# Streaming the two halves of split float32 activations as one 512-column matmul

## The chip, the cores and the metric

The kernel runs on one core of a Trainium2 chip, in one launch. The metric is the device time of that core in microseconds (us), lower is better. Three runs of the kernel before took 940.13 to 944.43 us, with a median of 941.47.

## The reference

Two layers of a decoder trunk on x of shape (1, 256, 1024), all float32. Each layer is, cut to what matters here:

```
xn = rms(x);  z = xn @ w_in                  # 1024 -> 7756 columns, split among the mixers and the gates
y_a = mlstm(silu(conv(z.mqk)), ...)          # 4 heads x 128, chunks of 128
y_b = dsa(top 64 of an indexer's scores)     # 8 heads x 64
y_c = diff_attn(...)                         # 4 heads x 128, two softmax maps
gates = sigmoid(z.g + b_gate)                # 3 x 1024
m = sum_b gates[b] * (y_b @ w_branch[b])     # 512 -> 1024, three times
x = x + m @ w_out                            # 1024 -> 1024
g, u = split(rms(x) @ w_gate_up)             # 1024 -> 2 x 2816
x = x + (silu(g) * u) @ w_down               # 2816 -> 1024
```

Every projection has to be as exact as float32 nearly is, so each float32 operand is split into a high part (rounded to the format that TensorE takes in one pass, float32r) and a low part (the rest). A product is then three passes: high x high, high x low and low x high.

## The kernel before

The 256 tokens are the columns of nearly everything. The weights of a layer are read in 151 chunks of at most 128 x 1024 numbers, in the fixed order of `plan()`: mLSTM q and k, the latent, the indexer, then queries, keys and values of the attentions and the mLSTM (512 columns each), 24 blocks of gates, 12 chunks of the branches, 8 of the output projection, 44 of gate and up, and 24 of the down projection. `chunk` (line 472) brings one in: a DMA into `raw`, a ScalarE copy into `whi` (the high part), a VectorE subtraction into `wlo` (the low part); each of the three has 3 buffers.

Two helpers multiply. `feat` (line 490) gives features as rows and the 256 tokens as columns: its stationary operand is a 128 x 128 block of weights, its moving operand the activations. An activation tile `a` is 128 x 2 x 256: `a[:, 0, :]` is the high part and `a[:, 1, :]` the low part, next to each other. Three matmuls of 256 columns follow each other: high weights with high activations, high weights with low activations, low weights with high activations. `tok` (line 497) gives tokens as rows; its moving operand is 256, 332 or 512 columns of weights. The change does not touch `tok`.

`feat` serves the mLSTM q and k (line 676, activations `xg`), the gates (line 1002, `xg`), the branches (line 1019, `y`), the output projection (line 1042, `mg`), gate and up (line 1052, `fx`) and down (line 1067, `h`). Its results go to tiles called `mm`, of which 4 exist, each one PSUM bank (2 KB per partition, 512 float32). A bank holds two groups of 256 columns side by side (two feature blocks) in the mLSTM, the gates, the branches and gate and up, and one group in the output and down projections. VectorE takes them out in one instruction, times 1/rms (`rB`), times the gate, or added to x.

The order of the work is not that of the code. `Order` records every instruction, and `schedule` puts them in an order by a list schedule: each engine takes the instruction that can start first, and among those of one time the one with the lowest number (its place in the code, less what `early` gives). `cost` (line 319) says how long an instruction lasts. Two instructions that touch one PSUM tile depend on each other even where they touch different halves, unless both only read. Each engine then runs its list strictly in that order, so a wait holds up all behind it. All instructions are issued at line 288, so the profile shows only that line and one has to go by the names of tiles. `K` is a tile of constants, `at` are the PSUM tiles of the attentions (4 more banks), `pad`, `cv` and `mqk` belong to the convolution, `gt` are gates, `mu` the gated branches, `gr` and `hf` the two halves of the feed-forward part, `dn` the down projection.

Of the kernel before, what the change touches and what calls it, by code (L numbers as in the profile page):

```python
# [11 lines left out]
F32 = mybir.dt.float32  # L12
# [7 lines left out]
class View:  # L20
    """A tile that is allocated when its first instruction is issued, or a part of it."""
# [96 lines left out]
class Order:  # L118
    """Records instructions, puts them in an order by a list schedule, and issues them in it."""
# [187 lines left out]
def lat(a, b):  # L307
    """From the end of an instruction on engine a to the start of one on b that reads it, in us."""
    if a == b:
        return {"tensor": 0.0, "vector": 0.127, "scalar": 0.15, "gpsimd": 0.13, "sync": 0.0}[a]  # L310
    if b == "tensor":
        return 0.25
    return 0.2 if a == "tensor" or "gpsimd" in (a, b) else 0.14
# [5 lines left out]
def cost(op, views):  # L319
    """The time of an instruction in us."""  # L320
    n = max(math.prod(v.shape[1:]) for v in views)
    psum = any(v.base.psum for v in views)
    if op.eng == "tensor":
        n = math.prod(views[0].shape[1:])
        if op.fn == "transpose":
            return 0.109
        if views[1].dtype == BF16:
            return n / 1200
        if views[1].dtype == F32R:
            return max(n, 256) / 2400 + 0.0024  # L330
        return 0.216 if n <= 128 else 4 * n / 2400 + 0.0048
    if op.eng == "scalar":
        t = (0.05 if psum else 0.092) + n * 0.00084
        extra = [op.kw.get("scale"), op.kw.get("bias"), op.kw.get("accum_out")]
        return t + 0.093 * sum(isinstance(v, View) for v in extra)
    if op.eng == "vector":
        if op.fn == "reciprocal":
            return 0.05 + n * 0.0063
        t = 0.065 + n * (0.00052 if op.fn in ("tensor_copy", "tensor_scalar") and not psum else 0.00104)
        if op.fn == "scalar_tensor_tensor":  # L340
            t += 0.061 * isinstance(op.args[2], View)
        if op.fn == "tensor_tensor_reduce":
            t += 0.061 * isinstance(op.args[3], View)
        if op.fn == "tensor_scalar":
            t += 0.061 * sum(isinstance(v, View) for v in op.args[2:4])
        return t
    if op.eng == "gpsimd":
        if op.kw.get("op") == OP.pow:
            return 0.3 + n * 0.165
        if op.fn == "memset":  # L350
            return 0.04 + n * 0.0005
        if op.fn in ("tensor_scalar", "tensor_copy"):
            return 0.16 + n * (0.0037 if any(isinstance(v, View) for v in op.args[2:4]) else 0.00083)
        return 0.15 + n * 0.0021
    return 0.02 + 128 * n * 4 / 365e3
# [26 lines left out]
def plan():  # L382
    """The order in which a layer's weights are read: (array, row blocks, col blocks)."""
    seq = []
    for f in range(8):
        seq.append([("in", k, O_QK + f * 128, 128) for k in range(8)])
    for a in range(2):
        seq.append([("in", k, O_CKV, 256) for k in range(4 * a, 4 * a + 4)])
    for ks in ((0, 1, 2), (3, 4, 5), (6, 7)):
        seq.append([p for k in ks for p in (("in", k, O_IQ, 324), ("in", k, O_IF, 8))])  # L390
    for a in range(4):
        seq.append([("in", k, O_SQ, 512) for k in (2 * a, 2 * a + 1)])
    for a in range(2):
        seq.append([("kv", k, 512 * a, 512) for k in range(2)])
    for o in (O_DQ, O_DK, O_DV, O_MV, O_MO):
        for a in range(4):
            seq.append([("in", k, o, 512) for k in (2 * a, 2 * a + 1)])
    for g in range(24):
        seq.append([("in", k, O_G + g * 128, 128) for k in range(8)])
    for b in BR:  # L400
        for ep in range(4):
            seq.append([("br%d" % b, k, ep * 256, 256) for k in range(4)])
    for e in range(8):
        seq.append([("out", k, e * 128, 128) for k in range(8)])
    for f in range(NFF):
        seq.append([("gu", k, f * 128, 128) for k in range(8)])
        seq.append([("gu", k, FF + f * 128, 128) for k in range(8)])
    for e in range(8):
        for ks in (range(0, 8), range(8, 16), range(16, 22)):
            seq.append([("dn", k, e * 128, 128) for k in ks])  # L410
    return seq
# [8 lines left out]
def kernel(ctx: ExitStack, tc: tile.TileContext, xT: bass.AP, wts: bass.AP, cst: bass.AP,  # L420
# [33 lines left out]
    # keeps TensorE's clock up until the first operands are there  # L454
# [35 lines left out]
    def feat(ps, w, c0, a, first, last):  # L490
        """ps [128 out, T] += w[:, c0:c0+128]^T a, three passes."""
        hi, lo = w
        PE.matmul(ps, hi[:, c0:c0 + 128], a[:, 0, :], start=first, stop=False)
        PE.matmul(ps, hi[:, c0:c0 + 128], a[:, 1, :], start=False, stop=False)
        PE.matmul(ps, lo[:, c0:c0 + 128], a[:, 0, :], start=False, stop=last)

    def tok(ps, w, c0, n, a, t, first, last):
        """ps [128 tok, n] += a[:, :, tile t]^T w[:, c0:c0+n], three passes."""
# [6 lines left out]
    def rsqrt_cols(t, n):  # L505
        """t <- t ** -0.5 on GpSimd (t [128, n])."""
        G.tensor_tensor(t, t, mhalf[:, :n], op=OP.pow)

    def norm(gcol, wide, first=False):
        """x*g as hi/lo parts, 1/rms as token columns [128, 2] and as rows [128, T]."""  # L510
# [63 lines left out]
    def swap_halves(ap):  # L574
        """[128, h, 64] seen with the halves of the last axis exchanged, as two views."""
        return ap[:, :, 32:64], ap[:, :, 0:32]

    def rot(dst, z, nh, a, b):
        """dst = z * a + swap(z) * b over nh heads; a, b [128, 64]."""
# [16 lines left out]
    def qk_heads(z, t, ab, dstT, query):  # L596
        """z [128 tok, 512] -> per-head RMS, RoPE, transposed into dstT[:, :, tile t]. Of a query
        the 1/rms is returned instead, as columns scaled by -1/sqrt(64), for softmax."""
# [20 lines left out]
    def softmax(t, heads, qT, kT, bias, scale):  # L619
        """exp(logits - max) of the heads, [128 q, len(heads), nk], and its row sums."""  # L620
# [16 lines left out]
    def keyT(p, n, t):  # L637
        """p [128 q, n, nk] -> [128 keys, n, key tile, 128 q]."""
# [8 lines left out]
    def parts(dst, ps, t, g=None):  # L647
        """hi/lo of ps [128, 4, 128] (scaled by g[:, k]) into dst[:, k, :, tile t]."""
# [11 lines left out]
    for li in range(L):  # L660
# [13 lines left out]
        # mLSTM q and k: projection, causal convolution, silu  # L674
        mqk = []
        for fp in range(4):
            ps = mmps([128, 2, T])
            for j in range(2):
                w = w_first if li == 0 and fp + j == 0 else chunk(li)
                for k in range(8):  # L680
                    feat(ps[:, j, :], w, k * 128, xg[k], k == 0, k == 7)
            qk = S.tile([128, 2, T], F32, tag="mqk", name="mqk", bufs=4)
            for j in range(2):
                f = 2 * fp + j
                pad = pads[j]
                with S.early(400):
                    V.tensor_mul(pad[:, 3:3 + T], ps[:, j, :], rB)
# [8 lines left out]
        # DSA latent  # L696
# [30 lines left out]
        # indexer projections and mLSTM gates  # L727
# [28 lines left out]
        # index scores and the top-k mask  # L756
# [25 lines left out]
        # DSA queries  # L782
# [15 lines left out]
        # DSA keys and values  # L798
# [15 lines left out]
        # DSA attention  # L814
# [19 lines left out]
        # differential attention  # L834
# [62 lines left out]
        # mLSTM gates  # L897
# [48 lines left out]
        # (s tile, t tile) blocks: (0, 0), (1, 1), (0, 1)  # L946
# [7 lines left out]
        # mLSTM values and output gate  # L954
# [44 lines left out]
        # branch gates  # L999
        gt = []  # L1000
        S.margin = MG
        for gp in range(12):
            ps = mmps([128, 2, T])
            for j in range(2):
                w = chunk(li)
                for k in range(8):
                    feat(ps[:, j, :], w, k * 128, xg[k], k == 0, k == 7)
            g = S.tile([128, 516], F32, tag="h", name="gt", bufs=22)[:, :512].rearrange("p (a t) -> p a t", a=2)
            with S.early(400):
                V.tensor_mul(g, ps, rB[:, None, :].to_broadcast([128, 2, T]))  # L1010
# [5 lines left out]
        # branch projections, gated and merged  # L1016
        mg = []
        us = [None] * 4
        for n, b in enumerate(BR):
            for ep in range(4):  # L1020
                w = chunk(li)
                ps = mmps([128, 2, T])
                for j in range(2):
                    for k in range(4):
                        feat(ps[:, j, :], w, k * 256 + j * 128, y[b][:, k], k == 0, k == 3)
                u = tmp([128, 2, T], "mu")
                V.scalar_tensor_tensor(u, gt[4 * b + ep], 1.0, ps, op0=OP.add, op1=OP.mult)
# [13 lines left out]
        # output projection  # L1041
        for e in range(8):
            w = chunk(li)
            ps = mmps([128, T])
            for k in range(8):
                feat(ps, w, k * 128, mg[k], k == 0, k == 7)
            V.tensor_add(x[e], x[e], ps)

        # SwiGLU
        xg, rcol, rB = norm(c[:, C_NF:C_NF + 8], True)  # L1050
        hs = []
        for f in range(NFF):
            ps = mmps([128, 2, T])
            for j in range(2):
                w = chunk(li)
                for k in range(8):
                    feat(ps[:, j, :], w, k * 128, xg[k], k == 0, k == 7)
            gr = tmp([128, T], "gr")
            V.tensor_mul(gr, ps[:, 0, :], rB)
            A.activation(gr, gr, AF.Silu)  # L1060
            hf = tmp([128, T], "hf")
            V.tensor_mul(hf, gr, ps[:, 1, :])
# [4 lines left out]
        for e in range(8):  # L1067
            ps = mmps([128, T])
# [5 lines left out]
            V.tensor_mul(d, ps, rB)  # L1074
# [26 lines left out]
def _layout(inp):  # L1101
    """The inputs in the kernel's layouts (moves only)."""
# [43 lines left out]
```

## Time and profile before

| | |
|---|---|
| runs, median (lowest to highest) | 941.47 us (940.13 to 944.43) |
| the profiled execution, first to last instruction | 942.7 us |
| matmuls | 7154 |
| HBM read | 158.27 MB, 169 GB/s over the span |

The page names no other time of the profiled execution than its span, which lies within the runs. An engine's busy share is an average over stages of very different kind; 16 DMA engines were busy for about half the span. Ends of matmuls are modelled: starts are what can be trusted.

### The profile page before, as it was taken

How to read it: one execution, taken by the hardware profiler on the slowest of the kernel's cores; microseconds unless marked ns; L12 is line 12 of the kernel's file. 1: busy time of each engine (PE TensorE's matmuls, PEld its weight loads, DVE VectorE, ACT ScalarE, POOL GpSimd, SP SyncE). 2: the span in 40 equal slices, each digit the busy share in tenths (PEclk: the TensorE clock that was granted, in tenths of full speed). 3: DMA queues.
4: the chain of work that ended last, by engine and by line, in shares of the span. 5: the costliest groups of instructions: out<-in, count | busy, mean ns of one | idle time of the engine just before them, and what ended most of it. 6: DMA issues, size and time to landing. Idle time of an engine off the chain costs nothing.

```text
span 942.7 us, 18057 instructions
## 1 busy us (share of the span) xinstructions
PE 933.5 (99%) x7154; PEld 888.6 (94%) x7154; DVE 678.6 (72%) x1268; ACT 534.0 (57%) x927; POOL 103.3 (11%) x149
## 2 busy tenths in 40 slices
PE   8999999999999999999999999999999999999998
PEld 7988779999999999999999787899999999999998
DVE  6889988765886666665578898796669866666553
ACT  5686667774365444444457767577644655445432
POOL 5002431110011000001110121213000300000000
PEclk9999999999999999999999999999999999999999
DMA  6655433445555555555555453333555555555663
GB/s 222 203 188 179 154 100 106 131 163 187 186 179 181 189 191 181 188 181 186 186 184 184 157 193 121 112 113 118 176 187 192 178 180 185 194 181 186 193 198 96
DMA packets 46821, 160.49 MB, mean 170 GB/s; under 512 B 5392, under 2 KB 7568, under 8 KB 46736
## 3 DMA queue, kind: packets, MB, share of 16 engines
q1 hardware_dynamic: 46736, 159.34, 52.0%
q8 instruction: 56, 0.92, 0.4%
q14 instruction: 29, 0.24, 0.1%
HBM read 158.27 MB, written 1.05 MB: 169 GB/s over the span
## 4 chain that ended last, share of the span: by engine, by line
PE 98%; DVE 1%; DMA 0%; issue 0%; SPq 0%; ACT 0%
PE mm L288 89%; PE at L288 8%; DVE e L288 0%; DMA x<-in_xT_dram 0%; DVE xg L288 0%; SPq L288 0%; DVE zr L288 0%; ACT xg L288 0%; DVE dn L288 0%; DVE x L288 0%; DVE rot L288 0%; ACT nsq L288 0%; DVE wlo L288 0%; DVE mn L288 0%; DVE cf L288 0%
## 5 line engine op out<-in xcount | busy, mean ns | idle before, releaser
L288 ACT ACTIVATE whi<-raw 128x1024 fp32r<-128x1024 f32 (+2 forms) x303 | 315.9, 1043 | 332.9 <-PE mm L288 212.0
L288 DVE TENSOR_TENSOR wlo<-raw,whi 128x1024 fp32r<-128x1024 f32 (+2 forms) x303 | 365.4, 1207 | 184.0 <-ACT whi L288 182.2
L288 PE MATMUL mm<-fx,whi 128*128 128x256 f32 x1408 | 249.6, 279 | 0.0
L288 PEld LDWEIGHTS mm<-fx,whi 128*128 128x128 f32 x1408 | 215.2, 188 | 0.0
L288 PE MATMUL mm<-xg,whi 128*128 128x256 f32 x1024 | 195.2, 289 | 1.8 <-DVE xg L288 1.8
L288 PE MATMUL mm<-fx,wlo 128*128 128x256 f32 x704 | 196.8, 280 | 0.0
L288 PEld LDWEIGHTS mm<-xg,whi 128*128 128x128 f32 x1024 | 163.7, 195 | 3.3 <-DVE xg L288 2.6
L288 PE MATMUL mm<-whi,xg 128*128 128x512 f32 (+2 forms) x512 | 150.3, 373 | 0.0
L288 PE MATMUL mm<-xg,wlo 128*128 128x256 f32 x512 | 148.0, 289 | 0.6 <-DVE wlo L288 0.6
L288 PEld LDWEIGHTS mm<-fx,wlo 128*128 128x128 f32 x704 | 132.0, 188 | 0.0
L288 PE MATMUL mm<-h,whi 128*128 128x256 f32 x704 | 124.5, 280 | 0.0
L288 PEld LDWEIGHTS mm<-h,whi 128*128 128x128 f32 x704 | 107.7, 188 | 0.0
L288 PEld LDWEIGHTS mm<-whi,xg 128*128 128x128 f32 x512 | 92.1, 188 | 14.7 <-issue 1.0
L288 PEld LDWEIGHTS mm<-xg,wlo 128*128 128x128 f32 x512 | 99.7, 195 | 1.2 <-DVE wlo L288 0.9
L288 PE MATMUL mm<-h,wlo 128*128 128x256 f32 x352 | 98.6, 280 | 0.0
L288 PE MATMUL mm<-wlo,xg 128*128 128x512 f32 (+2 forms) x256 | 95.6, 374 | 0.0
L288 PE MATMUL mm<-y,whi 128*128 128x256 f32 x384 | 67.9, 280 | 0.0
L288 PEld LDWEIGHTS mm<-h,wlo 128*128 128x128 f32 x352 | 66.4, 189 | 0.0
L288 POOL TENSOR_TENSOR nacc<-nacc,nsq 128x256 f32<-128x256 f32 x28 | 26.3, 939 | 361.1 <-ACT nsq L288 222.5
L288 PEld LDWEIGHTS mm<-y,whi 128*128 128x128 f32 x384 | 58.6, 187 | 0.0
L288 PEld LDWEIGHTS mm<-wlo,xg 128*128 128x128 f32 x256 | 48.3, 189 | 7.7 <-issue 0.7
L288 PE MATMUL mm<-y,wlo 128*128 128x256 f32 x192 | 53.6, 279 | 0.0
(193 smaller groups left out, 1095.4 us busy)
## 6 DMA issues: line engine op xcount, KB each, us to landing
raw<-in_wts_dram SPq DMA_DIRECT2D x279, 512.0 KB, 3.7
raw<-in_wts_dram SPq DMA_DIRECT2D x16, 384.0 KB, 3.9
raw<-in_wts_dram SPq DMA_DIRECT2D x4, 498.0 KB, 3.6
x<-in_xT_dram SPq DMA_DIRECT2D x4, 256.0 KB, 4.4
out_dram<-x SPq DMA_DIRECT2D x8, 128.0 KB, 3.4
row<-in_rows_dram SPq DMA_DIRECT2D x2, 388.0 KB, 5.7
raw<-in_wts_dram SPq DMA_DIRECT2D x2, 332.0 KB, 2.9
raw<-in_wts_dram SPq DMA_DIRECT2D x2, 256.0 KB, 3.8
```

The lines of the kernel that those rows point to most:

```text
L288: getattr(getattr(nc, o.eng), o.fn)(*args, **kw)
```

## The change

`feat` streams both halves of the activations, 512 columns, past one load of the high weights, into a whole bank: the products with the high activations into its first half, those with the low activations into its second. The low weights still meet the 256 high activations, into the first half. In the last call of a group the short pass comes first, so that the long one ends the group. A new helper `both` adds the two halves: a ScalarE copy of the second, then a VectorE addition of the first. Each group of 256 columns so needs a bank of its own, where two shared one. What was one instruction out of PSUM now works on the sum in SBUF; the output projection adds the two halves to x in two instructions. `cost` gives a pass 0.0115 us beside its stream, where it gave 0.0024.

```diff
         if views[1].dtype == F32R:
-            return max(n, 256) / 2400 + 0.0024
+            return max(n, 256) / 2400 + 0.0115
...
     def feat(ps, w, c0, a, first, last):
         hi, lo = w
-        PE.matmul(ps, hi[:, c0:c0 + 128], a[:, 0, :], start=first, stop=False)
-        PE.matmul(ps, hi[:, c0:c0 + 128], a[:, 1, :], start=False, stop=False)
-        PE.matmul(ps, lo[:, c0:c0 + 128], a[:, 0, :], start=False, stop=last)
+        if last:
+            PE.matmul(ps[:, 0, :], lo[:, c0:c0 + 128], a[:, 0, :], start=False, stop=False)
+        PE.matmul(ps, hi[:, c0:c0 + 128], a, start=first, stop=last)
+        if not last:
+            PE.matmul(ps[:, 0, :], lo[:, c0:c0 + 128], a[:, 0, :], start=False, stop=False)
+
+    def both(dst, ps):
+        A.activation(dst, ps[:, 1, :], AF.Copy)
+        V.tensor_add(dst, dst, ps[:, 0, :])
...
         for fp in range(4):
-            ps = mmps([128, 2, T])
+            ps = []
             for j in range(2):
                 w = w_first if li == 0 and fp + j == 0 else chunk(li)
+                ps.append(mmps([128, 2, T]))
                 for k in range(8):
-                    feat(ps[:, j, :], w, k * 128, xg[k], k == 0, k == 7)
+                    feat(ps[j], w, k * 128, xg[k], k == 0, k == 7)
...
                 with S.early(400):
-                    V.tensor_mul(pad[:, 3:3 + T], ps[:, j, :], rB)
+                    both(pad[:, 3:3 + T], ps[j])
+                    V.tensor_mul(pad[:, 3:3 + T], pad[:, 3:3 + T], rB)
...
         for gp in range(12):
-            ps = mmps([128, 2, T])
+            g = S.tile([128, 516], F32, tag="h", name="gt", bufs=22)[:, :512].rearrange("p (a t) -> p a t", a=2)
             for j in range(2):
                 w = chunk(li)
+                ps = mmps([128, 2, T])
                 for k in range(8):
-                    feat(ps[:, j, :], w, k * 128, xg[k], k == 0, k == 7)
-            g = S.tile([128, 516], F32, tag="h", name="gt", bufs=22)[:, :512].rearrange("p (a t) -> p a t", a=2)
-            with S.early(400):
-                V.tensor_mul(g, ps, rB[:, None, :].to_broadcast([128, 2, T]))
+                    feat(ps, w, k * 128, xg[k], k == 0, k == 7)
+                with S.early(400):
+                    both(g[:, j, :], ps)
+            V.tensor_mul(g, g, rB[:, None, :].to_broadcast([128, 2, T]))
...
-                ps = mmps([128, 2, T])
+                u = tmp([128, 2, T], "mu")
                 for j in range(2):
+                    ps = mmps([128, 2, T])
                     for k in range(4):
-                        feat(ps[:, j, :], w, k * 256 + j * 128, y[b][:, k], k == 0, k == 3)
-                u = tmp([128, 2, T], "mu")
-                V.scalar_tensor_tensor(u, gt[4 * b + ep], 1.0, ps, op0=OP.add, op1=OP.mult)
+                        feat(ps, w, k * 256 + j * 128, y[b][:, k], k == 0, k == 3)
+                    both(u[:, j, :], ps)
+                V.scalar_tensor_tensor(u, gt[4 * b + ep], 1.0, u, op0=OP.add, op1=OP.mult)
...
-            V.tensor_add(x[e], x[e], ps)
+            for j in range(2):
+                V.tensor_add(x[e], x[e], ps[:, j, :])
...
-            ps = mmps([128, 2, T])
+            gr, hf = tmp([128, T], "gr"), tmp([128, T], "hf")
             for j in range(2):
                 w = chunk(li)
+                ps = mmps([128, 2, T])
                 for k in range(8):
-                    feat(ps[:, j, :], w, k * 128, xg[k], k == 0, k == 7)
-            gr = tmp([128, T], "gr")
-            V.tensor_mul(gr, ps[:, 0, :], rB)
-            A.activation(gr, gr, AF.Silu)
-            hf = tmp([128, T], "hf")
-            V.tensor_mul(hf, gr, ps[:, 1, :])
+                    feat(ps, w, k * 128, xg[k], k == 0, k == 7)
+                both((gr, hf)[j], ps)
+                if j == 0:
+                    V.tensor_mul(gr, gr, rB)
+                    A.activation(gr, gr, AF.Silu)
+            V.tensor_mul(hf, gr, hf)
...
             d = tmp([128, T], "dn")
-            V.tensor_mul(d, ps, rB)
+            both(d, ps)
+            V.tensor_mul(d, d, rB)
             V.tensor_add(x[e], x[e], d)
```

## Rows read from the trace of the kernel before

**Rows 1.** The page: busy time of each engine, and the chain that ended last.

```profile
PE 933.5 (99%) x7154; PEld 888.6 (94%) x7154; DVE 678.6 (72%) x1268; ACT 534.0 (57%) x927; POOL 103.3 (11%) x149
...
PE 98%; DVE 1%; DMA 0%; issue 0%; SPq 0%; ACT 0%
```

**Rows 2.** Chain of waits in order of time: start us, us, what, instructions.

```profile
68.48 28.88 PE mm L288 x127
...
200.72 90.39 PE mm L288 x759
...
293.44 185.66 PE mm L288 x1574
```

**Rows 3.** Groups by form, low-weight passes: names, shape, count | busy us, mean ns | idle.

```profile
L288 PE MATMUL mm<-fx,wlo 128*128 128x256 f32 x704 | 196.8, 280 | 0.0
...
L288 PE MATMUL mm<-xg,wlo 128*128 128x256 f32 x512 | 148.0, 289 | 0.6 <-DVE wlo L288 0.6
...
L288 PE MATMUL mm<-h,wlo 128*128 128x256 f32 x352 | 98.6, 280 | 0.0
...
L288 PE MATMUL mm<-y,wlo 128*128 128x256 f32 x192 | 53.6, 279 | 0.0
...
L288 PE MATMUL mm<-mg,wlo 128*128 128x256 f32 x128 | 35.6, 283 | 0.0
```

**Rows 4.** Timeline of TensorE, mLSTM projection: start us, us, what, merged count.

```profile
17.17 0.63 PE L288 MATMUL mm<-xg,whi 128*128 128x256 f32 x2
...
17.81 0.63 PE L288 MATMUL mm<-xg,whi 128*128 128x256 f32 x2
...
20.86 0.40 PE L288 MATMUL mm<-xg,whi 128*128 128x256 f32 x2
...
21.22 0.40 PE L288 MATMUL mm<-xg,whi 128*128 128x256 f32 x2
```

**Rows 5.** Stretches: us, busy PE, PEld, DVE, ACT, POOL (instructions), PEclk, DMA, GB/s.

```profile
115.00:200.00 85.00, 85.00 (x636) 77.14 (x635) 68.00 (x188) 60.24 (x156) 18.62 (x35) 1.00 0.35 114
200.00:231.00 31.00, 31.00 (x261) 31.00 (x260) 18.50 (x22) 16.72 (x27) 0.00 (x0) 1.00 0.55 183
...
254.00:266.00 12.00, 12.00 (x104) 12.00 (x103) 11.62 (x20) 6.25 (x10) 0.00 (x0) 1.00 0.58 186
...
294.00:399.00 105.00, 105.00 (x894) 105.00 (x893) 66.08 (x94) 51.83 (x75) 0.00 (x0) 1.00 0.57 186
```

**Rows 6.** Groups by form, VectorE and ScalarE: mean ns is the second number.

```profile
L288 DVE TENSOR_TENSOR wlo<-raw,whi 128x1024 fp32r<-128x1024 f32 x279 | 341.8, 1226 | 180.9 <-ACT whi L288 179.2
...
L288 DVE SCALAR_TENSOR_TENSOR cv<-pad,col,cv 128x256 f32<-128x256 f32 x48 | 21.5, 483 | 0.1
...
L288 DVE SCALAR_TENSOR_TENSOR mu<-gt,mm 128x512 f32<-128x512 f32 x24 | 16.5, 686 | 8.2 <-PE mm L288 8.2
...
L288 DVE TENSOR_TENSOR x<-x,mm 128x256 f32<-128x256 f32 x16 | 6.6, 414 | 4.1 <-PE mm L288 4.1
...
L288 ACT ACTIVATE rB<-at 128x256 f32<-128x256 f32 x4 | 1.5, 385 | 7.9 <-PE at L288 7.9
```

**Rows 7.** Timeline of VectorE in the third branch: start us, us, what.

```profile
257.62 1.22 DVE L288 TENSOR_TENSOR wlo<-raw,whi 128x1024 fp32r<-128x1024 f32 x1
258.76 0.42 DVE L288 SCALAR_TENSOR_TENSOR mg<-mu,mg 128x256 fp32r<-128x256 f32 x1
259.09 0.42 DVE L288 TENSOR_TENSOR mu<-mu 128x256 f32<-128x256 f32 x1
259.43 0.68 DVE L288 SCALAR_TENSOR_TENSOR mu<-gt,mm 128x512 f32<-128x512 f32 x1
260.14 0.42 DVE L288 TENSOR_TENSOR mu<-mu 128x256 f32<-128x256 f32 x1
```

**Rows 8.** Timeline of VectorE behind the last matmul: start us, us, what, idle.

```profile
938.66 0.42 DVE L288 TENSOR_TENSOR dn<-mm,rB 128x256 f32<-128x256 f32 x1 [6.01 <-PE mm L288]
939.12 0.42 DVE L288 TENSOR_TENSOR x<-x,dn 128x256 f32<-128x256 f32 x1
```

More of the change, by code (lines that the diff above doesn't have):

```diff
@@ L1043 @@
             w = chunk(li)
-            ps = mmps([128, T])
+            ps = mmps([128, 2, T])
             for k in range(8):
                 feat(ps, w, k * 128, mg[k], k == 0, k == 7)
-            V.tensor_add(x[e], x[e], ps)
+            for j in range(2):
+                V.tensor_add(x[e], x[e], ps[:, j, :])
         xg, rcol, rB = norm(c[:, C_NF:C_NF + 8], True)
@@ L1052 @@
         for f in range(NFF):
-            ps = mmps([128, 2, T])
+            gr, hf = tmp([128, T], "gr"), tmp([128, T], "hf")
             for j in range(2):
                 w = chunk(li)
+                ps = mmps([128, 2, T])
                 for k in range(8):
-                    feat(ps[:, j, :], w, k * 128, xg[k], k == 0, k == 7)
-            gr = tmp([128, T], "gr")
-            V.tensor_mul(gr, ps[:, 0, :], rB)
-            A.activation(gr, gr, AF.Silu)
-            hf = tmp([128, T], "hf")
-            V.tensor_mul(hf, gr, ps[:, 1, :])
+                    feat(ps, w, k * 128, xg[k], k == 0, k == 7)
[4 more added lines that the diff above has]
+            V.tensor_mul(hf, gr, hf)
             h = S.tile([128, 516], F32R, tag="h", name="h", bufs=22)[:, :512].rearrange("p (a t) -> p a t", a=2)
@@ L1067 @@
         for e in range(8):
-            ps = mmps([128, T])
+            ps = mmps([128, 2, T])
             for ks in (range(0, 8), range(8, 16), range(16, 22)):
```

## The prediction

> **What bounds the kernel now.** I read the page first. TensorE is busy in 99% of the 942.7 us, VectorE in 72%, ScalarE in 57%, and the chain that ended last is 98% TensorE [rows 1]. The reader should distrust the 99%, since ends of matmuls are modelled and overlap, so I went to the chain of waits in order of time, where a piece is a stretch in which TensorE waited for nobody. Its pieces give the true step from one pass to the next: 185.66 us for 1574 passes of 256 columns is 118.0 ns, 90.39 us for 759 is 119.1 ns, and 28.88 us for 127 passes of 512 columns is 227.4 ns [rows 2]. The granted clock is 1.00, the 2.4 GHz level, in every stretch [rows 5]; there 256 columns stream in 106.7 ns and 512 in 213.3 ns. So a pass of 256 pays 11 to 12 ns beside its stream and one of 512 pays 14 ns: nearly the same sum for twice the columns. TensorE issues without gaps, and only fewer or cheaper steps shorten the kernel, as long as the other engines still keep ahead of it.
>
> The view by stretches then says where they might not. In the gate and up projections of the feed-forward part VectorE is busy 66.1 of 105 us, and 18.5 of 31 in the gate projections after attention. But in the last third of the branch projections it is busy 11.62 of 12 us, and in the attention stretch 68.0 of 85 [rows 5].
>
> **What the change removes.** The number of `feat` calls is that of the passes with low weights: 704 + 512 + 352 + 192 + 128 = 1888 [rows 3]. Each has three steps now, and gets one of 512 and one of 256 instead. For activations in `xg` three steps then take 0.36 us (20.86 to 21.22) [rows 4], for `mg` I take the same; for `fx`, `h` and `y` 3 x 118 = 354 ns [rows 2]. After it is 227 + 120 = 347 or 227 + 118 = 345. That is 13 ns for 640 calls (8.3 us) and 9 ns for 1248 (11.2 us), 19.5 us; some 20 calls run in the first 18.6 us, where three steps take 0.64 us (17.17 to 17.81) [rows 4], 213 ns each, which is 256 columns at the 1.2 GHz level with nothing beside the stream, so they gain nothing, and I take off 0.3: **19.2 us**. Bounds: if the long pass pays only the 11.3 ns that the short one does, it is 640 x 13.3 + 1248 x 11.3 = 22.6 us; if 512 columns cost what two passes of 256 cost, nothing. The row of 512 columns is of the same array and number format, so I stay by it. One weight load fewer per call lies inside these steps, as loads run beside the matmuls.
>
> A page of the Trainium skill speaks against this: TensorE: Matmul & The Clock Gate (Back-to-back issue gap) gives the isolated step at full clock as the stream plus about 2.5 ns. By it the change would save 1888 x 2.5 = 4.7 us, an estimate. The trace does not agree for this number format: 11 to 14 ns lie beside the stream [rows 2, 4].
>
> **What it adds.** Each group of columns must now be put together: a ScalarE copy of one half from PSUM (256 columns: 385 ns) and a VectorE addition of the other (414 ns) [rows 6]. What was one VectorE instruction out of PSUM (times 1/rms, times a gate) stays, now on SBUF. Groups per layer: 8 mLSTM, 24 gates, 24 branch halves, 44 gate and up, 8 down; the 8 of the output projection get only a second addition. So per layer 108 copies and 116 additions, over both layers 216 x 0.385 = 83 us of ScalarE and 232 x 0.414 = 96 us of VectorE. As shares of the span both fit (VectorE to 82%). What matters is each stage, with VectorE's true rate, from start to start: 1.14 us for a low weight part of 1024 columns, 0.34 for 256 columns, 0.71 for the 512-column product with its gate [rows 7]. A chunk of weights (8 calls) will take TensorE 8 x 0.346 = 2.77 us.
>
> Gate and up projections, in the stretch of 105 us with 38 groups: VectorE 66.1 + 38 x 0.414 = 81.8, ScalarE 51.8 + 38 x 0.385 = 66.4, of some 102 [rows 5, 6]: hidden. Down projection: one group per 22 calls, hidden. Gate projections: 2 x 1.14 + 2 x 0.34 + 0.71 = 3.7 of 5.5 us, hidden. In the attention stretch, gate groups run as filler and bring VectorE some 13 x 0.34 = 4.4 us, and the mLSTM groups ahead of it 8 x 0.34 = 2.7; VectorE still has 12.5 us free in the gates that follow [rows 5], so the end of attention may slip by 7 us without TensorE running dry. I put 1 us there for both layers, bounds 0 and 7.
>
> mLSTM chunk: the three steps of the convolution, 0.483 us each [rows 6], would stand about 0.40 apart, as 0.414 stands 0.34 apart: 1.14 + 0.34 + 0.34 + 3 x 0.40 = 3.0 us of VectorE against 2.77, a lag of 2 us over 8 chunks. A lag is paid only when PSUM is full. Four banks rotate; one held two groups, now it holds one. A group of 8 calls lasts 2.77 us, so three later groups can run before the bank is needed: hidden.
>
> Branch projections, for one chunk (two groups of four calls, 1.38 us each): first branch 1.14 + 0.68 + 0.71 = 2.5 us, hidden; second, with another 512-column addition, 3.24, over by 0.47, times 4 is 1.9; third, with two additions and two low parts of `mg` (about 0.34 each), 1.14 + 0.68 + 0.71 + 0.68 + 0.67 = 3.88, over by 1.1, times 4 is 4.4. VectorE thus lags by 6.3 us at the end. Four banks bear three groups, 4.15 us, less the copy, the addition and two handoffs of some 0.2: 3.0 us. When the last chunk needs its bank the lag is 1.9 + 3.3 = 5.2: **TensorE waits 2.2 us.** Then the output projection needs the last `mg`: about 3 us of lag left, its own 3.9 and two low weight parts queued ahead (2.3) make 9.2 us after the last branch pass. Meanwhile TensorE can do 3 chunks x 6 calls x 0.345 = 6.2 us, minus what banks deny: **a wait of about 2.5.** Together 4.7 us a layer, **9.4 us**; bounds 0 (the order written by the list schedule is redone with these costs and may spread the additions) and the rival below.
>
> End: after the last matmul stand now two VectorE instructions at 938.66 and 939.12, then the output's transfer [rows 8]. A copy (0.39) and another VectorE step (0.46) come in: **0.9 us** with nothing to hide it. The seam between the layers gets the same, but there each half of a group pair has a bank of its own, so TensorE has more calls to fill it: 0.
>
> **Sum**, against the profiled execution's 942.7 us span: -19.2 + 9.4 + 0.9 + 1.0 = -7.9, so 934.8. The runs' median, 941.47, lies 1.2 lower and the span between lowest and highest, so I expect a median of 941.5 - 7.9 = 933.6; I write 933.5.
>
> **Rivals.**
> Everything is hidden: the new order keeps VectorE ahead in the branch stage, only the end's 0.9 us stays. For it: the stage before is gapless although VectorE is busy 97% there [rows 5]. Against: the work added there exceeds what is free. 941.5 - 19.2 + 0.9 = 923.2, with the better long pass 919.8.
>
> VectorE sets the pace, and the kernel gets slower: if its instructions cost their full recorded durations (1.226, 0.414, 0.686, 0.483 us [rows 6]) because each now waits for a ScalarE copy just before it, a branch chunk of the second kind takes 1.23 + 0.83 + 0.69 + 0.69 = 3.44 and of the third 4.4, over by 4 x 0.67 + 4 x 1.65 = 9.3; an mLSTM chunk 3.5, over by 8 x 0.73 = 5.8. Twice 15.1 is 30.2, less 19.2, plus 0.9: 953.4. It decides from the point where the waits in these two stages pass 18.3 us. Against: instructions are issued closer than their durations now [rows 7].
>
> The long pass saves nothing: 512 columns take 236 ns. Then 941.5 + 11.3 = 952.8. Against: 227 ns over 127 steps. The isolated-step rule above is its milder form: 941.5 - 4.7 + 11.3 = 948.1.
>
> **How the numbers follow.** Forecast (928 to 939) 0.46; everything hidden (919 to 928) 0.22; VectorE's pace, in whole or part (939 to 954) 0.20; no saving 0.07; the milder form 0.05. Less than 0.5%, some 4.7 us, can't be told from no change. Below 936.8 lie 0.40 of the forecast and all of the second: 0.62. Above 946.2 lie the last two but 0.01 and 0.09 of VectorE's pace: 0.20. The rest is 0.18. The range 919 to 949 leaves out 0.07 for no saving and about 0.08 of VectorE's pace.
>
> **What would show it.** Step of the long pass in gapless pieces: 225 to 228 ns if right, 236 if the third rival is. Feed-forward stretches of 105 us should shrink by 2.5 to 3% with no waits. Waits of TensorE for `mu` or for a bank at the end of the branch stage, and for `mg` at the start of the output projection, some 5 us a layer: if none, the second case; if they begin in the second branch and show in the mLSTM stage too, VectorE's pace. Two more instructions after the last matmul. The prediction is wrong if TensorE's gaps lie in attention or in the feed-forward part.

## The result, and the profile after

The changed kernel takes 955.0 us (median of 4 runs, 954.8 to 956.2) against 940.8 for the kernel before (median of 4 runs, 936.3 to 944.4): a ratio of 1.0148, interval 1.0101 to 1.0196. It is slower; faster was forecast. The profiled executions span 954.4 and 942.7 us, so the traces have 11.7 of the 14.2 us to explain. The kernel before took 935.0 to 945.5 us in the job of the first four experiments and 943.7 to 945.4 in the two later jobs, and no trace shows what sets its shorter runs apart, so ratios of different jobs can be some tenths of a per cent off against each other.

The page of the changed kernel, engines and the chain that ended last [rows 1]:

```profile
PE 931.8 (98%) x5266; PEld 796.1 (83%) x5266; DVE 760.6 (80%) x1500; ACT 592.8 (62%) x1143; POOL 109.5 (11%) x149
...
PE 19%; DVE 0%; POOL 0%; ACT 0%; issue 0%; POOLq 0%
```

1888 matmuls are gone, a quarter, and TensorE is as busy as ever. VectorE is at 80%, where 82 was forecast. The chain now reaches back only 19% of the span, to a GpSimd step at the start of the last feed-forward part: there TensorE had waited, where before it had hardly waited at all.

The end of the chain of waits (start us, us, what, instructions), for [rows 2, 8]:

```profile
765.23 0.73 POOL nacc L288
...
768.33 181.22 PE mm L288 x1030
...
949.56 0.39 ACT dn L288
...
949.98 0.43 DVE dn L288
...
950.44 0.44 DVE dn L288
...
950.90 0.42 DVE x L288
```

181.22 us for 1030 passes is 175.9 ns, or 351.9 for a long and a short one. Three short ones took 3 x 118.0 = 353.9 in the kernel before [rows 2]. So in the feed-forward part a call saves 2 ns, where 9 were forecast. Behind the last matmul stand four instructions instead of two, as forecast.

TensorE's waits, all of 0.6 us and more but the start's `warm` (us in all, times, longest):

```profile
PE mm L288 <- DVE mu L288: 5.2, 4, 1.3
PE mm L288 <- DVE xg L288: 3.1, 3, 1.5
...
PE at L288 <- POOL nacc L288: 2.2, 2, 1.1
PE at L288 <- DVE mn L288: 1.7, 4, 0.6
PE mm L288 <- DVE wlo L288: 1.0, 1, 1.0
PE mm L288 <- ACT whi L288: 0.8, 2, 0.4
PE mm L288 <- ACT zc L288: 0.6, 1, 0.6
PE at L288 <- POOL rcol L288: 0.6, 1, 0.6
```

Before there were 1.8 for `xg`, 0.6 for `wlo` and 0.3 for `mn`, and no others are listed. The two lines for `mu` and `nacc` belong to the seam between branches and feed-forward part, where the waits were forecast. TensorE at the seam of layer 0 (start us, us, what, idle before):

```profile
265.85 0.39 PE L288 MATMUL mm<-y,whi 128*128 128x512 f32 x1
267.54 0.47 PE L288 MATMUL mm<-mg,whi 128*128 128x512 f32 x1 [1.30 <-DVE mu L288]
...
269.79 0.77 PE L288 MATMUL mm<-mg,whi 128*128 128x512 f32 x1 [1.31 <-DVE mu L288]
270.35 0.41 PE L288 MATMUL mm<-mg,wlo 128*128 128x256 f32 x1
270.56 1.05 PE L288 MATMUL mm<-mg,whi 128*128 128x512 f32 x2
...
276.25 0.28 PE L288 MATMUL mm<-mg,wlo 128*128 128x256 f32 x1
276.37 0.40 PE L288 MATMUL mm<-mg,whi 128*128 128x512 f32 x1
```

and VectorE beside it:

```profile
265.70 0.76 DVE L288 SCALAR_TENSOR_TENSOR mg<-mu,mg 128x256 fp32r<-128x256 f32 x2
266.38 0.69 DVE L288 SCALAR_TENSOR_TENSOR mu<-gt,mu 128x512 f32<-128x512 f32 x1
266.98 0.42 DVE L288 TENSOR_TENSOR mu<-mu,mm 128x256 f32<-128x256 f32 x1
267.41 1.23 DVE L288 TENSOR_TENSOR wlo<-raw,whi 128x1024 fp32r<-128x1024 f32 x1
268.56 0.75 DVE L288 TENSOR_TENSOR mu<-mu 128x256 f32<-128x256 f32 x2
269.23 0.42 DVE L288 TENSOR_TENSOR mu<-mu,mm 128x256 f32<-128x256 f32 x1
```

Both waits end 0.14 us after an addition `mu<-mu,mm`, the new instruction that empties a bank (266.98 + 0.42, 269.23 + 0.42), while `mg` was written before. So TensorE waits for a bank both times. VectorE has no gap in these 4 us: it is the engine that lags. After the second wait the steps double: 213 ns for 256 columns (270.35 to 270.56) and 427 for 512, until 275.9; at 276.25 they are 117 again. That is the 1.2 GHz level, and the stretches say the same (us, busy PE, PEld, DVE, ACT, POOL, granted clock, DMA share, GB/s) [rows 5]:

```profile
254.00:266.00 12.00, 12.00 (x70) 10.41 (x68) 12.00 (x21) 7.37 (x15) 0.00 (x0) 1.00 0.64 198
264.00:276.00 12.00, 9.39 (x37) 7.58 (x36) 11.02 (x25) 5.27 (x13) 0.00 (x0) 0.72 0.42 131
294.00:399.00 105.00, 103.92 (x591) 90.26 (x590) 80.42 (x131) 61.17 (x111) 2.19 (x3) 1.00 0.58 185
...
735.00:747.00 12.00, 9.39 (x52) 7.56 (x50) 10.75 (x26) 5.15 (x10) 0.00 (x0) 1.00 0.32 90
```

The last row is the same place in layer 1, with the same two waits of 1.30 and 1.31 us: there the clock stays at 1.00, and 52 passes run where layer 0 has 37.

From the starts of the first pass over `y`, `mg`, `fx` and `h` and of the last one over `h`, both layers together, against what the prediction's terms give for each stage:

| stage (us, change against before) | predicted | measured |
|---|---|---|
| up to the branches | -6.7 + 0.3 + 1.0 = -5.4 | +1.4 - 0.4 = +1.0 |
| branches, output projection, the `nacc` wait | -3.4 + 9.4 = +6.0 | layer 0: 1.28 + 4.55 + 1.08; layer 1: 1.29 + 1.79 + 1.14; +11.1 |
| rest of the feed-forward part | 1056 x 9 ns = -9.5 | gate and up -0.1, down -1.3; -1.4 |
| tail | +0.9 | +0.9 |
| sum | -8.0 | +11.6, of 11.7 between the spans |

### The profile page after: what moved, and what is told of

Same layout as the page of the kernel before. It is cut to its first block, busy times and chain, and to the rows that moved or that the text cites. A ratio compares the mean times of both kernels' runs of the same rounds, so it can differ in the third digit from the quotient of the medians.

```text
span 954.4 us, 14999 instructions
## 1 busy us (share of the span) xinstructions
PE 931.8 (98%) x5266; PEld 796.1 (83%) x5266; DVE 760.6 (80%) x1500; ACT 592.8 (62%) x1143; POOL 109.5 (11%) x149
## 3 DMA queue, kind: packets, MB, share of 16 engines
HBM read 158.27 MB, written 1.05 MB: 167 GB/s over the span
## 5 line engine op out<-in xcount | busy, mean ns | idle before, releaser
L288 PE MATMUL mm<-fx,whi 128*128 128x512 f32 x704 | 242.4, 397 | 0.0
L288 PE MATMUL mm<-xg,whi 128*128 128x512 f32 x512 | 182.1, 404 | 3.2 <-DVE xg L288 3.1
L288 PE MATMUL mm<-fx,wlo 128*128 128x256 f32 x704 | 183.8, 281 | 0.0
L288 PEld LDWEIGHTS mm<-fx,whi 128*128 128x128 f32 x704 | 126.4, 188 | 23.8
L288 PE MATMUL mm<-xg,wlo 128*128 128x256 f32 x512 | 136.4, 287 | 1.0 <-DVE wlo L288 1.0
L288 PE MATMUL mm<-h,whi 128*128 128x512 f32 x352 | 122.5, 395 | 0.0
L288 PEld LDWEIGHTS mm<-xg,whi 128*128 128x128 f32 x512 | 94.1, 191 | 21.6 <-DVE xg L288 4.2
L288 PEld LDWEIGHTS mm<-h,whi 128*128 128x128 f32 x352 | 65.2, 188 | 14.2
L288 PE MATMUL mm<-y,whi 128*128 128x512 f32 x192 | 64.4, 396 | 0.0
L288 PE MATMUL mm<-mg,whi 128*128 128x512 f32 x128 | 47.3, 418 | 6.0 <-DVE mu L288 5.2
```

The lines of the kernel that those rows point to most:

```text
L288: getattr(getattr(nc, o.eng), o.fn)(*args, **kw)
```

## Experiments

Ratios are to the kernel before in the same job, with their 95% interval. The changed kernel stands at 1.0148.

**Which part costs the time: the sums, the place of the sums, or the merged pass?** Four kernels of one job.

All long passes of a weight chunk first, then its short ones:

```diff
+        for i, (c0, a) in enumerate(blocks):
+            PE.matmul(ps, hi[:, c0:c0 + 128], a, ...)
+        for c0, a in blocks:
+            PE.matmul(ps[:, 0, :], lo[:, c0:c0 + 128], a[:, 0, :], ...)
```

> Edit: the long passes of a chunk (8, 4 or 6) follow each other, then its short ones; same passes, same sums. Theory A (alternation: a long pass costs 234 ns where 227 was forecast only because a short pass stands before or after it): inside a train long passes step at 227 ns, short ones at 107 to 118, and the kernel comes 8 to 13 us under the changed one, about 944 us. Theory B (the activations as moving operand, with weights as stationary one, cost that much in any order): the long pass stays at 232 to 236 ns and the time at 955 +- 2 us.

Measured: 1.0153 (1.0100 to 1.0206), no change. The last piece is 180.95 us for 1032 passes, 350.7 ns for a pair against 351.9. Turning between lengths isn't where the gain went, in the feed-forward part.

The long pass as two passes of 256, everything else as changed:

```diff
-        PE.matmul(ps, hi[:, c0:c0 + 128], a, start=first, stop=last)
+        PE.matmul(ps[:, 0, :], hi[:, c0:c0 + 128], a[:, 0, :], start=first, stop=False)
+        PE.matmul(ps[:, 1, :], hi[:, c0:c0 + 128], a[:, 1, :], start=False, stop=last)
```

> Edit: the long pass again as two passes of 256 columns, into the two halves of the bank; sums and banks as in the changed kernel. Theory 1 (the merging saves next to nothing: 236 against 234 ns): 955 + 1888 x 2 ns = about 959 us, at most 961. Theory 2 (the merging does save 9 to 13 ns a call, and what was lost lies elsewhere): 955 + 19 = about 974 us.

Measured: 1.0172 (1.0109 to 1.0235). Merging by itself is worth some 2 us (1.7 by the medians, 956.67 against 955.0 of another job; 0.24% by the ratios), which these intervals don't tell from nothing. The trace does better. The last piece of its chain:

```profile
767.71 182.79 PE mm L288 x1546
```

That is 118.2 ns a pass, 354.7 a call: merging saves 2.8 ns in the feed-forward part.

Without the sums; this leaves the product of high weights and low activations out of the output:

```diff
-                both((gr, hf)[j], ps)
...
-                    V.tensor_mul(gr, gr, rB)
+                    V.tensor_mul(gr, ps[:, 0, :], rB)
...
```

> Leaves out the product of high weights with low activations from what is taken out of PSUM: the passes are those of the changed kernel, one bank per group, but the second half is never read, so ScalarE's copy and VectorE's extra addition are gone. Theory 1 (the putting together costs all of the loss): back to 937 to 941 us, no waits at the seam from branches to output projection. Theory 2 (the loss lies in TensorE's steps or its clock): 950 us or more.

Measured: 0.9968 (0.9942 to 0.9995). So all that the merged passes and the new cost line bring, with no price for the sums, is 3.0 us, and no more than 5.5 by the interval; 19.2 were expected of the passes. (The two profiled executions, 935.0 and 942.7 us, differ by 7.7; the spread of the kernel before lies between the two figures.) The sums cost the rest, 1.8% or 17 us; the branches take 33.8 us, the output projection 22.5, and TensorE waits for neither `mu` nor `nacc`.

Branches and output projection as before, the rest as changed:

```diff
+                ps = mmps([128, 2, T])
                 for j in range(2):
-                    ps = mmps([128, 2, T])
                     for k in range(4):
-                        feat(ps, w, k * 256 + j * 128, y[b][:, k], k == 0, k == 3)
-                    both(u[:, j, :], ps)
+                        feat3(ps[:, j, :], w, k * 256 + j * 128, y[b][:, k], k == 0, k == 3)
...
```

> Edit: branches and output projection as before the change (three passes of 256, one instruction out of PSUM); merged passes elsewhere. Theory 1 (the loss sits at the seam of these two stages, 35.2 + 27.6 and 35.2 + 24.8 us where they took 33.9 + 23.0): 9 us are won back, about 946 us, and no half-rate passes near 270 us. Theory 2 (VectorE's added load everywhere, or the tails): 952 us or more.

Measured: 1.0043 (1.0016 to 1.0070). The seam thus costs 1.05%, 9.9 us, by the ratios and 11.4 by the medians (955.0 and 943.56), beside the little its merged passes save. The longest of TensorE's waits in this kernel, but the start's `warm`:

```profile
PE mm L288 <- DVE xg L288: 2.6, 3, 1.5
...
PE at L288 <- DVE mn L288: 1.7, 4, 0.6
...
```

The others listed are `wlo` with 0.8, `zc` and `rcol` with 0.6 each: `mu` and `nacc` are gone together. The wait of GpSimd's sum at the start of the feed-forward part is an echo of the seam.

**The cost line, the gates, the clock.** The kernel before with nothing but the new cost line:

```diff
-            return max(n, 256) / 2400 + 0.0024
+            return max(n, 256) / 2400 + 0.0115
```

> The kernel before with one line of the change alone: a pass costs 0.0115 us beside its stream in the list schedule, where it cost 0.0024. Theory 1 (this line only makes the plan truer): within 0.5% of before, 936 to 944 us. Theory 2 (the new plan is itself a part of the loss): 944 to 950 us.

Measured: 1.0021 (1.0012 to 1.0030). The line alone costs 2 us. 0.0115 gives 118.2 ns for 256 columns, which is the true step; so the truer price makes the kernel slower. The loss lies for the most part in no wait. The longest pieces without one, in the feed-forward parts, read

```profile
295.22 186.29 PE mm L288 x1574
...
758.22 183.02 PE mm L288 x1547
```

and in the kernel before, for the second beside that of [rows 2]:

```profile
756.74 181.89 PE mm L288 x1545
```

That is 118.3 ns a pass in both layers, where it was 118.0 and 117.7, with the same three passes to a call. Branches and feed-forward parts are 2.2 us longer by it, of 2.5 between the two spans; the way to the branches is 1.8 us longer in layer 0 and 1.3 shorter in layer 1. Why passes that wait for nothing get dearer in another order is not shown. (A tile is allocated when its first instruction is issued, so another order may also put the buffers elsewhere; no run tests that.)

Merged passes and sums in the gate projections alone, with the new cost line:

```diff
-                    feat(ps[:, j, :], w, k * 128, xg[k], k == 0, k == 7)
+                    featm(ps, w, k * 128, xg[k], k == 0, k == 7)
...
+                    both(g[:, j, :], ps)
```

> The kernel before, with merged passes, own banks and the sum in the gate projections alone (384 of 1888 calls), and the new cost line. There a call took 360 ns in three steps and takes 352 in two. Theory 1 (merging pays where the steps were 120 ns and where the sum is hidden): 384 x 8 ns = 3 us under before, 935 to 939 us. Theory 2 (the gate sums slow the attention beside which they run): 940 us or more.

Measured: 0.9993 (0.9984 to 1.0001). 384 calls at 8 ns are 3.1 us; less the 2 us of the line, 1.1 are left. Measured are 0.7, which the interval doesn't tell from nothing.

The changed kernel with 24 matmuls that nobody reads ahead of each output projection:

```diff
+        dm = atps([128, T])
+        for _ in range(24):
+            PE.matmul(dm, mg[1][:, 0, 0:128], mg[1][:, 0, :], start=True, stop=True)
```

> The changed kernel with 24 idle passes of 256 columns per layer (their result is not used) that need an early merged tile only and so may run where TensorE waits at the seam from branches to output projection. Theory 1 (after the wait TensorE runs some 5 us at its lower clock, which costs 2.5 us or more in the layer where it happens): the granted clock stays at 1.00 between 262 and 280 us and the time falls to 951 to 953. Theory 2 (the clock is an effect that costs nothing, the loss is the wait itself): 955 us or, with the idle passes on the path, up to 958.

Measured: 1.0085 (1.0071 to 1.0099). 48 matmuls more make the kernel faster: 953.05 us (950.4 to 954.0), where the changed kernel, not timed in this job, took 955.0 (954.8 to 956.2). Its stretch at the seam of layer 0:

```profile
264.00:276.00 12.00, 11.61 (x71) 9.87 (x70) 10.75 (x25) 5.63 (x11) 0.00 (x0) 1.00 0.25 87
```

The clock is 1.00 and 71 passes run instead of 37 (some of them idle ones). Branches and output projection of layer 0 take 59.97 us together against 62.80; in layer 1, which had kept its clock, 59.99 against 60.05. So the low clock cost 2.8 us there.

Another 2.8 us between the two traces lie ahead of the branches of layer 0 (first branch pass at 229.5 against 232.3), and most of them are the clock's doing too. From the first pass over `ckv`, near 64 us, the 950 passes up to the branches come in the same order in both traces. 1.2 us come from the first 21 us, where VectorE lets TensorE go 0.4 us later in the changed kernel and its clock rises some 2 us later (steps of 427 ns end at 19.9 us, not at 18.0); the other 1.6 come between 148 and 153 us. There the changed kernel's stretch reads, behind a wait of 0.61 us for `mn`,

```profile
148.00:154.00 6.00, 6.00 (x27) 4.56 (x26) 4.66 (x23) 4.53 (x16) 0.20 (x1) 0.72 0.00 0
```

while this run has the same wait, a clock of 1.00 and 36 passes. What the clock takes also differs from one execution to the next. With series of passes behind its end (`e_micro`, below), the changed kernel shows no fall at 148 us, and at the seams, with the same two waits of 1.30 and 1.31 us, it shows one in both layers:

```profile
265.00:277.00 12.00, 10.17 (x48) 8.65 (x49) 9.20 (x24) 4.08 (x10) 0.00 (x0) 0.86 0.26 87
...
733.00:745.00 12.00, 10.42 (x49) 8.80 (x49) 9.17 (x23) 4.04 (x10) 0.00 (x0) 0.86 0.23 82
```

**What sets the step of a long pass?** First TensorE alone, in series of 40 passes behind the end of the changed kernel, 512 columns with weights as stationary operand and tiles of `y`'s buffers moving, or the other way round:

```diff
+    run("ma", [(w(i), F[:, i % 8, :]) for i in range(N)])
+    run("mb", [(w(i), F[:, 0, :]) for i in range(N)])
+    run("mc", [(w(0), F[:, i % 8, :]) for i in range(N)])
...
```

> The changed kernel with eight short series of passes behind its last addition (they add some 60 to 80 us), TensorE alone at work: 40 passes of 512 columns with weights as stationary and activations as moving operand, both changing (ma), moving operand fixed (mb), stationary fixed (mc), both fixed (md), the changed kernel's alternation of 512 and 256 (me), three of 256 as before (mf), and the roles of `tok` (mg2, mh). Theory A (the step of the long pass depends on its operands or their places): ma at 232 to 236 ns, mg2 at 227. Theory B (the extra 7 ns come from the other engines' traffic in the kernel): all series of 512 at 227 ns or less, the alternation at 227 + 118. Theory C (the pair 512 + 256 has a price of its own): ma at 227, me at 350 or more.

Measured, in the chain of waits (start us, us, what, instructions):

```profile
965.84 9.33 PE mb L1115 x40
...
993.84 7.29 PE me L1115 x41
1001.14 7.57 PE mf L1115 x62
1008.71 9.32 PE mg L1115 x40
```

9.33 / 40 = 233 ns, whichever operand changes, and also with the roles exchanged (series `mg`, the `mg2` of the expectation, for which theory A had 227). `me`, long and short in turn, takes 353 a pair; `mf`, three of 256, 3 x 118.4. So other engines, waits or changing operands do not make the 233. It is the step itself, and 227, on which the forecast stood, had to be the special case. In the trace of before both can be read, in the same form and the same helper (start us, us, what):

```profile
68.78 0.63 PE L288 MATMUL mm<-whi,ckv 128*128 128x512 f32 x2
...
70.88 0.40 PE L288 MATMUL mm<-whi,ckv 128*128 128x512 f32 x1
...
85.18 0.61 PE L288 MATMUL mm<-whi,xg 128*128 128x512 f32 x2
...
87.90 0.39 PE L288 MATMUL mm<-whi,xg 128*128 128x512 f32 x1
```

Between the first two starts lie 9 passes over `ckv`: 233.3 ns. Between the last two lie 12 over `xg`: 226.7. `ckv` is allocated in the buffers of `y` and `fx`, `mg` in those of `xg`. Hence one more kernel, with series of 48 out of both:

```diff
+    run("na", [(w(i), f(i)) for i in range(N)])
+    run("nb", [(w(i), x(i)) for i in range(N)])
+    run("nc", [(x(i // 3)[:, 0:128], W[:, 512 * (i % 2):512 * (i % 2) + 512]) for i in range(N)])
+    run("nd", ... ((w(i), x(i)), (l(i), x(i)[:, 0:256])) ...)
...
```

> The changed kernel, with eight series of 48 passes put behind its end, in which TensorE has nothing else beside it: na, stationary in a weight buffer, moving 512 columns out of the buffers that y and fx use; nb, the same with moving tiles out of the buffers that xg and mg use; nc, stationary out of the xg buffers, moving 512 columns of weights (the form that took 227 ns in the kernel before); nd, 512 columns and 256 in turn out of the xg buffers; ne and nf, 256 columns out of the xg and the y buffers; ng and nh, as nb with one operand fixed. Theory 1, the buffer sets the step: nb, nc, ng and nh take 227 ns and na 233, ne takes 120 and nf 118. Theory 2, the work around sets it: all series of 512 columns take 233 and both of 256 take 118. For nd both leave room: 347 ns for the two if the long one keeps its 227 beside a short one, 352 as in the changed kernel if turning between two lengths is what costs it the 6 ns.

Measured:

```profile
971.75 10.91 PE nb L1114 x48
982.66 10.88 PE nc L1114 x48
993.54 8.93 PE nd L1114 x50
1002.47 6.21 PE ne L1114 x50
1008.68 6.14 PE nf L1114 x50
1014.83 10.89 PE ng L1114 x48
...
```

`nb`, `nc`, `ng` and `nh` take 227 ns, moving or stationary; the steps of `na`, once its clock is up, are 235 and 232 in turn. `ne`, less the two passes of 512 at its ends, is (6.21 - 0.46) / 48 = 119.8 ns, and `nf` (6.14 - 0.47) / 48 = 118.1. Theory 1 holds, for TensorE alone: the buffer that an activation tile lies in sets the step, and that of `xg` is the dearer one for 256 columns and the cheaper one for 512. `nd` gives (8.93 - 0.45) / 24 = 353 a pair: turning between the two lengths costs the `xg` tiles the 6 ns that they gain in a train. What it is about the place of the buffers stays open.

**A version that beats both?** The gates alone, now with the old cost line; and the same with the long passes of a chunk grouped.

```diff
-            return max(n, 256) / 2400 + 0.0115
+            return max(n, 256) / 2400 + 0.0024
```

> The kernel before with the long pass in the gate projections alone and with the old cost line (0.0024). The 384 calls of the gates save 8 ns each, 3.1 us or 0.33%, if nothing waits for their sums. Theory 1, the cost line costs its 0.2% whatever it is added to: 0.9993 of the run with the new line less 0.0021, so 0.997 of the time before. Theory 2, the loss by the cost line is an accident of one order of work: about 0.9993 again, or anything between 0.995 and 1.002.

> As the gates alone with the old cost line, and with the 8 long passes of a chunk ahead of its 8 short ones. With xg tiles such trains of long passes fell from 235 to 227 ns after some five passes, and the short ones behind them took about 118.6: a call then takes some 348.7 ns against 360 before and 351.8 in turn. Theory 1: 384 x 11 ns = 4.3 us are saved, 0.9955 of the time before. Theory 2, the trains of eight lose at their ends what they gain inside (with all stages grouped the time did not move): as ungrouped, 0.997 to 0.999.

Measured: 0.9971 (0.9960 to 0.9982) and 0.9962 (0.9950 to 0.9975). Both beat the kernel before, by 2.7 and 3.6 us. The first is what theory 1 gave (0.997), a value that theory 2 left room for; the interval of the second holds the marks of both its theories (0.9955 and 0.997), and the two kernels aren't told apart from each other. TensorE's waits in the first, beside `warm` and 0.6 us for `wlo`:

```profile
PE mm L288 <- DVE xg L288: 1.8, 2, 1.2
PE at L288 <- DVE mn L288: 0.6, 2, 0.3
...
```

Where VectorE has slack the sums are free, and the 8 ns come out nearly whole (2.7 of 3.1 us, interval 1.7 to 3.8).

The changed kernel with the old cost line, in the same job (the same diff):

> The changed kernel with the old cost line (0.0024 beside the stream). Theory 1, the line is a part of the loss of its own, 0.2% as in the kernel before: 1.0148 becomes 1.0127. Theory 2, with the sums added the true price of a pass helps the planner: 1.015 or more. The seam's waits (1.3 us at the end of the branches, 1.8 to 4.6 more in the output projection) should stay under both.

Measured: 1.0135 (1.0121 to 1.0149), where theory 1 said 1.0127 and theory 2 1.015 or more; the interval of 1.0148 is too wide to settle it. The waits for `mu` are shorter here (3.0 us, longest 0.6), but the branches take 35.7 us, and the way to them in layer 1 is 4.7 us longer than in the changed kernel, 3.0 of it a wait for `pad` that the changed kernel doesn't have: another order of work moves losses about, and the sum stays.

## Why the prediction was wrong

**The step that failed** is the first term: "That is 13 ns for 640 calls (8.3 us) and 9 ns for 1248 calls (11.2 us)", with its ground "The row of 512 columns is of the same array and number format, so I stay by it." The row [rows 2] was of 127 passes, all but some 11 of them over `xg`. In all other buffers the long pass takes 233 ns, and beside a short one it takes 234 with `xg` too. Measured, the 640 calls save 8 ns (360 to 352, medians 120 and 234 with 117 to 118) and the 1248 about 2: 5.1 + 2.5 = 7.6 us, an estimate from these steps, instead of 19.2. The trace that the prediction was made from held the counter-row, the passes over `ckv` (48 in all, 233 ns where they run without a gap). The bounds given were right, 0 to 22.6; the value between them was taken from the one form of 512 columns that was looked at. The third rival's mark, 236 ns, was nearer than the forecast's 225 to 228.

The rule that the page of the Trainium skill gives (TensorE: Matmul & The Clock Gate, Back-to-back issue gap) would have given 2.5 ns a call. The feed-forward part agrees in size, with 2.0 to 2.8, though not in kind: 11 ns lie beside the stream of 256 columns and 20 beside that of 512.

**The seam** was right in place and cause, VectorE's lag, and in its sum. 4.7 us a layer were forecast, 2.2 for a bank and 2.5 for `mg`. Measured are 2.6 for a bank, none for `mg`, 0.4 for `whi`, and 1.1 for `nacc` at the next stage, which was not foreseen: 4.1. That the sums lie so near each other is in part luck, since one of the two forecast waits isn't there and another stands in its place. What the sum lacked was the clock, 2.8 us more in layer 0 of the profiled execution, which the idle passes take away.

**Up to the branches** 1.0 was put for attention and mLSTM with a bound of 7. The stage came out 6.4 us worse than forecast: 512 calls at 5 ns less are 2.6 of it, and 1.6 are the low clock between 148 and 153 us in the profiled execution. 2.2 stay. The cost line is a part: alone it makes this stage 1.8 us longer in layer 0 and 1.3 shorter in layer 1, single executions both, and the prediction priced it at nothing, here and in the branches and the feed-forward part, where it costs 2.2. The waits that are new here (`mn`, `zc`, `rcol`) are each 0.6 to 1.7 us. How these shares split stays open.

**Feed-forward part:** "shrink by 2.5 to 3% with no waits" failed with the step; it shrank by 0.4%, and its start got the echo. 2.0 ns a call are what is left against the kernel before; against the same kernel with two passes of 256, which has the new cost line too, it is 2.8. That the sums there are hidden was right: 181.22 us run without a wait. **Tail:** 0.9 forecast, 0.9 measured.

Of the rivals, VectorE's pace came within 2 us of the time, but not by its mechanism: the mLSTM stage, which it named, shows no such waits. The third rival (952.8), a long pass that saves nothing beside the forecast waits, came as near and was nearer in the mechanism. The time is the sum of a small saving, a seam near its forecast, a low clock at the seam and in the attention of layer 0, and a cost line that makes gapless passes dearer.

## What to carry to other kernels

Before a saving per instruction is multiplied by a thousand, read the step from every group of that form in the trace, by operand, and not from the first gapless piece: here 227 and 233 ns stood in the same trace, and the difference was most of the forecast. Passes over 512 columns saved 2 to 8 ns a call over two of 256; work that another engine must do for them has to be free, so put such a change where that engine has slack (the gates: 0.9971) and leave it out where it has none (the seam: +1.05%). A constant of a planner is a change of its own, to be timed alone. Before a difference between two traces is put down to the order of the work, compare the order and the granted clock of the stretch: here 1.6 us with the very same order were the clock.

## What the runs showed of the hardware

With TensorE alone and the same instruction, the step depended on the buffer of the activation tile, in either role: 512 columns took 227 ns out of one set and 233 out of another, 256 columns 119.8 and 118.1, the other way round.

Two waits of 1.3 us, 2.25 us apart, were followed by some 6 us at the 1.2 GHz level in layer 0 (granted clock 0.72 over 12 us), and the same two waits in layer 1 by none; in another execution of the same passes they were followed by a shorter fall in both layers (0.86 over 12 us each). A single wait of 0.61 us stood before a fall in attention in one run (0.72 over 6 us, 27 passes) and before none in another with the same order of passes (1.00, 36 passes). What tells these cases apart was not shown.
